# Two value projections from the unnormalised input, ahead of the norm

## The chip, the cores and the metric

The kernel runs on one core of a Trainium2 chip. The metric is the device time in microseconds of one execution; the runs of the kernel before have a median of 806.23 us.

## The reference

Two stacks of layers on x of 256 tokens and 1024 features, in float32. What is around the change is the first of them, an even layer:

```python
def rms_norm(x, g):
    xf = x.astype(f32)
    y = xf * lax.rsqrt(jnp.mean(xf * xf, axis=-1, keepdims=True) + EPS)
    return (y * g.astype(f32)).astype(x.dtype)

def even_layer(x, g_norm, w_in, b_f, w_out):
    z = rms_norm(x, g_norm) @ w_in
    qa, ka, va, ga, fa, qb, kb, vb, gb = jnp.split(z, cuts, axis=-1)
    log_f = jax.nn.log_sigmoid(fa.astype(f32) + b_f.astype(f32))
    ya = forgetting_attention(hA(qa), hA(ka), hA(va), log_f)   # 16 heads of 64, causal, decayed by cumsum(log_f)
    yb = dilated_attention(hB(qb), hB(kb), hB(vb))             # 16 heads of 64, three dilations
    y = jnp.concatenate([ya * jax.nn.silu(ga), yb * jax.nn.silu(gb)], axis=-1)
    return x + y @ w_out
```

Behind it come a retention layer with a norm and 4 heads, a layer with a state-space mixer beside sliding-window attention, and a gated feed-forward layer. Since the norm's factor is one number for each token, it can be multiplied on a product's rows instead of on x.

## The kernel before

All products are kept at float32 precision by splitting each operand into a high part (rounded to float32r) and a low part (the rest), and by three matmuls: high x high, high x low, low x high. The class `Weights` holds the list of all weight tiles (128 x 1024, 0.52 MB each) in the order in which they are used. `load` issues one tile's DMA on SP's queue into one of five raw buffers; `_prepare` casts it to the high part on ACT (L102) and takes the low part as a subtraction on DVE (L107), or on POOL for every n-th tile where a share is given to `plan`; `next` hands out a tile and prepares two ahead. The six pairs of prepared buffers hold what TensorE uses.

The start: x is loaded in two row tiles of two halves each (`load_x`), the gain row is spread over the partitions by TensorE (L636), and `norm_transposed` takes the squares (L232 on ACT, L229 on DVE), the factor (L217, L221 on POOL), multiplies x by factor and gain (L245), transposes on TensorE (L265), and splits into `xTh` and `xTl` (L272 on ACT, L273 on DVE). The second row tile's transposes are put behind the second matmul of the first product by `second_tile`. `first_xs` (L327, L334) is that first product, the v projection of the first eight forgetting heads: 48 matmuls of 512 columns.

Then the loop over the two kinds of heads (`m`: forgetting, dilated), two halves of eight heads (`hf`) and two groups of four heads (`i`): v by `proj_xs` (L312 to L316), the forget gates once (`forget_gates`, L281 to L283, a scan, and a store of the sums to DRAM at L678), then q, k and the gate by `proj_ws` (L293, L294; evacuated by ACT and DVE at L297 to L301), and for each pair of heads the scores (L376), masks read back from DRAM (`fox_masks`, L683 to L687), `masked_min` (L384, L386), exponentials, transposes (L400) and the product with v (L410). A product bank of kind `pp` exists three times, `at` twice, `pt` twice, `py` once. The tables of the state-space mixer (`tables_common`, L453 ff.) stand in the program behind the fourth group and are put earlier by the scheduler: each engine's instructions are laid out by a simulated timeline at build time, by priority and readiness, and then run in that order on the engine. On SP's queue the DMAs are in the same way in one fixed order.

Of the kernel before, what the change touches and what calls it, by code (L numbers as in the profile page):

```python
# [36 lines left out]
KE = ("pp", "py")  # L37
XH = 2
# [7 lines left out]
class Weights:  # L46


    def __init__(self, tc, raw, par, ahead):
        self.tc, self.nc, self.raw, self.par, self.ahead = tc, tc.nc, raw, par, ahead  # L50
        self.after, self.loaded, self.loads, self.lows = [], [], 0, []
        self.jobs, self.shares, self.done, self.used, self.ready = [], [], [], 0, {}

# [25 lines left out]
    def load(self):  # L79
        while self.loads in self.ready:  # L80
            self.loads += 1
        ap = self.jobs[self.loads]
        self.loads += 1
        r = self.raw.tile([P, 1024], F32, tag="raw", name="wraw")
        self.nc.sync.dma_start(r[:, :ap.shape[1]], ap)
        self.loaded.append(r)

    def _prepare(self):
# [13 lines left out]
        i = nc.scalar.copy(h[:, :n], r[:, :n])  # L102
# [5 lines left out]
        self.done.append((h, lo))  # L108

# [19 lines left out]
def model_kernel(ctx: ExitStack, tc: tile.TileContext, a: dict, out: bass.AP):  # L129
# [23 lines left out]
    g_row = nrm.tile([P, D], F32, tag="gain", name="g_row")  # L153
    nc.sync.dma_start(g_row[:1, :], a["even_norm"])
    x = [res.tile([P, D], F32, name=f"x{t}") for t in range(2)]

    def load_x(t):
        for h in range(XH):
            sl = slice(h * D // XH, (h + 1) * D // XH)
            nc.sync.dma_start(x[t][:, sl], a["x"][t * P:(t + 1) * P, sl])  # L160

    load_x(0)
# [9 lines left out]
    for m in ("a", "b"):  # L172
        for hf in range(2):
            w.plan(xs("w_v" + m, hf), SH[0] if m + str(hf) != "a0" else 2)
            if m == "a" and hf == 0:
                w.plan(ws("w_fa", 0))
# [24 lines left out]
    w.load()  # L201
    load_x(1)
# [32 lines left out]
    def norm_transposed(t, g, th, tl, name, kinds=("pt", "pt"), eng=None, after=None):  # L235

        with tc.high_priority():
            xt = x[t]
            parts = [mean_square(xt[:, h * 512:(h + 1) * 512], D, name, eng if h else None) for h in range(2)]
            r = rstd_from(parts, EPS, name)  # L240
            xn = []
            for h in range(2):
                sl = slice(h * 512, (h + 1) * 512)
                xn.append(nrm.tile([P, 512], F32, tag="xn", bufs=3, name="xn"))
                V.scalar_tensor_tensor(xn[h], xt[:, sl], r, g[h], op0=ALU.mult, op1=ALU.mult)  # L245
            return transposed(xn, 8, th, tl, 0, t, kinds, after)

# [11 lines left out]
    def transposed(src, n, th, tl, k0, t, kinds=("pt", "pt"), after=None):  # L259

        m = min(4, n)
        for b, sb, kind in zip(range(0, n, 4), src, kinds):
            pt = bank(kind)
            for j in range(m):
                i = T.transpose(pt[:, j * P:(j + 1) * P], sb[:, j * P:(j + 1) * P], ident)  # L265
                if after is not None:
                    tc.add_manual_dep(i.ins, after.ins.name, NOSYNC, reason="order")
                    after = None
# [49 lines left out]
    def first_xs(mid):  # L318

        tiles = [w.next() for _ in range(4)]  # L320
        ps = [bank("pp"), bank("pp")]
        for t in range(2):
            st = slice(t * P, (t + 1) * P)
            for g in range(0, 8, 2):
                for xp in (xTh, xTl):
                    for k in range(g, g + 2):
                        m = T.matmul(ps[t], xp[:, k, st], tiles[k // 2][0][:, 512 * (k % 2):512 * (k % 2) + 512],  # L327
                                     start=xp is xTh and k == 0, stop=False)
                        if t == 0 and xp is xTh and k == 1:
                            mid(m)  # L330
        for t in range(2):
            st = slice(t * P, (t + 1) * P)
            for k in range(8):
                T.matmul(ps[t], xTh[:, k, st], tiles[k // 2][1][:, 512 * (k % 2):512 * (k % 2) + 512],  # L334
                         start=False, stop=k == 7)
# [117 lines left out]
    def tables_common(pool, scratch):  # L453
# [7 lines left out]
        nc.sync.dma_start(sp, a["ssm_par"])  # L461
# [172 lines left out]
    g_even = [bank("at") for h in range(2)]  # L634
    for h in range(2):
        T.matmul(g_even[h], ones[:1, :], g_row[:1, h * 512:(h + 1) * 512], start=True, stop=True)  # L636
    norm_transposed(0, g_even, xTh, xTl, "e0", eng=V)

    def second_tile(after):
        norm_transposed(1, g_even, xTh, xTl, "e1", KE, None, after)  # L640

    lctx = ExitStack()
    ypool = lctx.enter_context(tc.tile_pool(name="ypool", bufs=1))
# [5 lines left out]
    yh, yl = y_tiles()  # L649
    with tc.tile_pool(name="ev", bufs=2) as ev, tc.tile_pool(name="evc", bufs=1) as evc, \  # L650
# [7 lines left out]
        def forget_gates():  # L658

            nc.sync.dma_start(bf, a["even_b_f"])  # L660
            nc.sync.dma_start(masks, a["c_masks"])
# [27 lines left out]

        for mi, m in enumerate(("a", "b")):  # L690
            for hf in range(2):
                ps = proj_xs(xTh, xTl, 8) if mi or hf else first_xs(second_tile)
                v = ev.tile([P, 2, 512], F32, tag="v", name="v")
                for t in range(2):
                    A.mul(v[:, t, :], ps[t], 0.5)
                if mi == 0 and hf == 0:
                    forget_gates()
                for i in range(2):
                    qk = []
# [3 lines left out]
                    proj_ws(k)  # L703
# [572 lines left out]
```

## Time and profile before

| | |
|---|---|
| runs, median | 806.23 us |
| profiled execution | 805.28 us, its span from first to last instruction 803.5 us |
| TensorE busy | 776.5 us (97%) |
| DVE, ACT, POOL busy | 592.8, 434.5, 202.0 us |
| granted TensorE clock, mean over the span | 0.992 |
| HBM | 162.9 MB moved, mean 203 GB/s |

The span is what the profile sees; the rest of the execution's time lies around it. Busy TensorE time is from pipelined matmuls whose ends are modelled, so that start-to-start distances say more of pace than durations do.

### The profile page before, as it was taken

How to read it: one execution, taken by the hardware profiler on the slowest of the kernel's cores; microseconds unless marked ns; L12 is line 12 of the kernel's file. 1: busy time of each engine (PE TensorE's matmuls, PEld its weight loads, DVE VectorE, ACT ScalarE, POOL GpSimd, SP SyncE). 2: the span in 40 equal slices, each digit the busy share in tenths (PEclk: the TensorE clock that was granted, in tenths of full speed). 3: DMA queues.
4: the chain of work that ended last, by engine and by line, in shares of the span. 5: the costliest groups of instructions: out<-in, count | busy, mean ns of one | idle time of the engine just before them, and what ended most of it. 6: DMA issues, size and time to landing. Idle time of an engine off the chain costs nothing.

```text
span 803.5 us, 12168 instructions
## 1 busy us (share of the span) xinstructions
PE 776.5 (97%) x4282; PEld 638.2 (79%) x4282; DVE 592.8 (74%) x1126; ACT 434.5 (54%) x783; POOL 202.0 (25%) x261
## 2 busy tenths in 40 slices
PE   7989999999999999999999999998898999999996
PEld 5867887877887778888888887796587888888886
DVE  7987677878888459796958666578759977786433
ACT  5875665665666347554444445627446655654431
POOL 4653111005405302201212003142233233223110
PEclk9999999999999999999999999999899999999999
DMA  8686553643844699985536395992333755555431
GB/s 296 215 276 231 170 171 119 222 153 123 270 163 146 199 337 388 358 288 196 192 123 210 123 323 177 326 357 93 124 124 110 238 192 184 183 185 183 157 131 53
DMA packets 55488, 162.91 MB, mean 203 GB/s; under 512 B 6385, under 2 KB 12801, under 8 KB 55426
## 3 DMA queue, kind: packets, MB, share of 16 engines
q1 hardware_dynamic: 55426, 162.12, 59.3%
q8 instruction: 34, 0.56, 0.3%
q14 instruction: 28, 0.23, 0.1%
HBM read 145.83 MB, written 16.27 MB: 202 GB/s over the span
## 4 chain that ended last, share of the span: by engine, by line
PE 83%; DVE 9%; DMA 3%; issue 3%; ACT 1%; SPq 0%; POOLq 0%; POOL 0%; DVEq 0%; ACTq 0%
PE bpp L293 19%; PE bpp L312 12%; PE bpp L313 12%; PE bpp L316 11%; PE bpp L294 10%; PE bat L293 5%; PE bat L294 2%; DVE wl L107 2%; PE bpy L410 2%; PE bpt L400 2%; PE bat L376 2%; DMA sr<-in_w_glu 1%; PE bat L955 1%; PE bpt L265 1%; DMA wraw<-in_w_v 1%
## 5 line engine op out<-in xcount | busy, mean ns | idle before, releaser
L107 DVE TENSOR_TENSOR wl<-wraw,wh 128x1024 fp32r<-128x1024 f32 x214 | 272.2, 1287 | 89.7 <-ACT wh L102 89.3
L102 ACT CAST wh<-wraw 128x1024 fp32r<-128x1024 f32 (+1 forms) x225 | 230.9, 1045 | 123.2 <-PE bpp L316 38.8
L293 PE MATMUL bpp<-xT,wh 128*128 128x512 f32 x672 | 242.6, 402 | 4.1 <-DVE q L301 4.1
L294 PE MATMUL bpp<-xT,wl 128*128 128x256 f32 x672 | 191.1, 284 | 0.0
L293 PEld LDWEIGHTS bpp<-xT,wh 128*128 128x128 f32 x672 | 126.9, 189 | 35.2 <-DVE q L301 4.7
L294 PEld LDWEIGHTS bpp<-xT,wl 128*128 128x128 f32 x672 | 127.6, 190 | 1.9 <-issue 1.2
L313 PE MATMUL bpp<-wl,xT 128*128 128x512 f32 (+1 forms) x288 | 109.4, 385 | 2.4 <-DVE wl L107 2.4
L312 PE MATMUL bpp<-wh,xT 128*128 128x512 f32 (+1 forms) x288 | 110.1, 389 | 0.1
L316 PE MATMUL bpp<-wh,xT 128*128 128x512 f32 (+1 forms) x288 | 75.3, 383 | 0.5 <-DVE xT L365 0.5
L313 PEld LDWEIGHTS bpp<-wl,xT 128*128 128x128 f32 x288 | 54.8, 190 | 13.6 <-DVE wl L107 3.8
L312 PEld LDWEIGHTS bpp<-wh,xT 128*128 128x128 f32 x288 | 54.6, 190 | 12.8 <-issue 1.5
L316 PEld LDWEIGHTS bpp<-wh,xT 128*128 128x128 f32 x288 | 52.2, 189 | 11.3 <-DVE xT L365 0.9
L293 PE MATMUL bat<-xT,wh 128*128 128x512 f32 x160 | 57.1, 399 | 0.0
L312 PE MATMUL bpp<-wh,yh 128*128 128x512 f32 x128 | 50.5, 400 | 0.0
L313 PE MATMUL bpp<-wl,yh 128*128 128x512 f32 x128 | 50.3, 396 | 0.0
L107 POOL TENSOR_TENSOR wl<-wraw,wh 128x1024 fp32r<-128x1024 f32 x11 | 27.4, 2492 | 85.5 <-ACT wh L102 85.5
L294 PE MATMUL bat<-xT,wl 128*128 128x256 f32 x160 | 45.0, 281 | 0.0
L293 PEld LDWEIGHTS bat<-xT,wh 128*128 128x128 f32 x160 | 30.1, 188 | 7.4
L316 PE MATMUL bpp<-wh,yl 128*128 128x512 f32 x128 | 35.7, 398 | 0.0
L393 ACT ACTIVATE s<-s,nm 128x128 f32<-128x128 f32 x40 | 15.8, 396 | 27.9 <-DVE nm L384 20.2
L294 PEld LDWEIGHTS bat<-xT,wl 128*128 128x128 f32 x160 | 30.2, 189 | 0.0
L1158 POOL TENSOR_TENSOR gr<-gr,Rh 128x512 f32<-128x512 f32 x10 | 19.8, 1980 | 38.4 <-ACT th L1157 38.4
(392 smaller groups left out, 1285.7 us busy)
## 6 DMA issues: line engine op xcount, KB each, us to landing
wraw<-in_w_o SPq DMA_DIRECT2D x36, 512.0 KB, 4.3
wraw<-in_w_gate SPq DMA_DIRECT2D x22, 512.0 KB, 3.7
wraw<-in_w_up SPq DMA_DIRECT2D x22, 512.0 KB, 3.4
wraw<-in_w_dn SPq DMA_DIRECT2D x22, 512.0 KB, 4.0
wraw<-in_w_v SPq DMA_DIRECT2D x16, 512.0 KB, 5.6
wraw<-in_w_g SPq DMA_DIRECT2D x16, 512.0 KB, 4.8
wraw<-in_w_q SPq DMA_DIRECT2D x12, 512.0 KB, 4.9
wraw<-in_w_va SPq DMA_DIRECT2D x8, 512.0 KB, 6.0
```

The lines of the kernel that those rows point to most:

```text
L102: i = nc.scalar.copy(h[:, :n], r[:, :n])
L107: self.lows.append(eng.tensor_tensor(lo[:, :n], r[:, :n], h[:, :n].bitcast(F32), op=ALU.subtract))
L293: T.matmul(ps, h, xT2[:, k].rearrange("p a b -> p (a b)"), start=k == 0, stop=False)
L294: T.matmul(ps[:, :S], l, xTh[:, k, :], start=False, stop=k == 7)
L312: T.matmul(ps, lh[:, k0 + k, st], wh, start=first and k == 0, stop=False)
L313: T.matmul(ps, lh[:, k0 + k, st], wl, start=False, stop=False)
L316: T.matmul(ps, ll[:, k0 + k, st], wh, start=False, stop=last and k == n - 1)
L376: i = T.matmul(ps[j][:, o], q[rows, qs], k[rows, ks], start=True, stop=True)
L393: A.activation(p[:, :P], s[:, :P], AF.Exp, bias=nm[:, 0:1], scale=-1.0, accum_out=dn[:, 0:1])
L400: T.transpose(pt[:, j * P:(j + 1) * P], p[:, j * P:(j + 1) * P], ident)
L410: i = T.matmul(o[64 * j:64 * j + 64], v[:, b, vc], src, start=b == 0, stop=b == 1)
L1158: G.tensor_tensor(two(gr), two(gr), rep2(Rh), op=ALU.mult)
```

## The change

x comes in a second time, transposed on the host (`xT`, eight blocks of 128 features by 256 tokens), and the even gain as a column for each block. The unnormalised, gained blocks are split at once into `xuh` and `xul` (in the buffer that later holds y's high part). Both v projections of the forgetting heads are computed from them: `first_xs` for the first half, group by group as blocks and weights arrive, then `proj_xs` for the second half in the banks of kind `at`; their evacuation multiplies by the factor of each token (`rh`, with the 0.5 that stood there before). Meanwhile `normalised` sums squares over the blocks, reduces them over the partitions with two small matmuls, spreads the factors over the partitions with two more, and writes the normalised `xTh` and `xTl` for the gates, q, k, g and the dilated heads' v. The first four weight tiles go into the buffer of y's low part, so nine raw tiles can be in flight; the first of them is loaded and cast in two halves. Three matmuls on ones run before anything has landed. x itself, the masks and the state-space parameters are issued later. All splits of these first weights are DVE's.

```diff
+        if self.loads in self.given:
+            r = self.given.pop(self.loads)
+        else:
+            r = self.raw.tile([P, 1024], F32, tag="raw", name="wraw")
+        parts = 2 if self.loads == 0 else 1
...
+        if not self.done:
+            nc.scalar.copy(h[:, :n // 2], r[:, :n // 2])
+            i = nc.scalar.copy(h[:, n // 2:n], r[:, n // 2:n])
...
+    def issue_after(self, n, i):
+
+        self.tc.add_manual_dep(i.ins, self.issued[n].ins.name, NOSYNC, reason="order")
...
+    warm = bank("py")
+    for n in (4, 4, 2):
+        T.matmul(warm[:, :n * P].rearrange("p (a b) -> p a b", a=n), ones, ones[:, None, :].to_broadcast([P, n, P]),
+                 start=True, stop=True)
+    warm = const.tile([P, 1], F32, name="warm")
+    A.copy(warm, ones[:, :1])
...
     def load_x(t):
...
+        w.issue_after(10, nc.sync.dma_start(x[t], a["x"][t * P:(t + 1) * P, :]))
...
-            w.plan(xs("w_v" + m, hf), SH[0] if m + str(hf) != "a0" else 2)
-            if m == "a" and hf == 0:
+            if m == "b":
+                w.plan(xs("w_vb", hf), SH[0])
+            elif hf == 0:
+                for h in range(2):
+                    w.plan(xs("w_va", h), SH[0])
                 w.plan(ws("w_fa", 0))
...
+    xu = ypool.tile([P, 16, S], F32R, tag="yh", name="xu")
+    xuh, xul = (xu.rearrange("p (k j) s -> p k j s", j=2)[:, :, j, :] for j in range(2))
+    early = ypool.tile([P, 16, S], F32R, tag="yl", name="early")[:].rearrange("p a b -> p (a b)").bitcast(F32)
+    w.given = {j: early[:, 1024 * j:1024 * j + 1024] for j in range(4)}
+    w.between = lambda: load_xT(1, 1)
+    for k in (2, 4, 6):
+        w.load()
+        load_xT(k)
+    for _ in range(5):
+        w.load()
...
-    def norm_transposed(t, g, th, tl, name, kinds=("pt", "pt"), eng=None, after=None):
...
+    def first_xs():
+
+
         ps = [bank("pp"), bank("pp")]
...
+        for g in range(0, 8, 2):
+            tiles.append(w.next())
+            part(g, xuh, 0, first=g == 0)
+            part(g, xul, 0)
+            if g:
+                part(g - 2, xuh, 1)
+        part(6, xuh, 1, last=True)
         return ps
...
-        nc.sync.dma_start(sp, a["ssm_par"])
+        w.issue_after(12, nc.sync.dma_start(sp, a["ssm_par"]))
...
-    g_even = [bank("at") for h in range(2)]
-    for h in range(2):
-        T.matmul(g_even[h], ones[:1, :], g_row[:1, h * 512:(h + 1) * 512], start=True, stop=True)
-    norm_transposed(0, g_even, xTh, xTl, "e0", eng=V)
...
+    for k in range(8):
+        xk = xT[k // 4][:, k % 4, :]
+        A.activation(xuh[:, k, :], xk, AF.Copy, scale=g_col[:, k:k + 1])
+        V.scalar_tensor_tensor(xul[:, k, :], xk, g_col[:, k:k + 1], xuh[:, k, :].bitcast(F32),
+                               op0=ALU.mult, op1=ALU.subtract)
...
+        def square_sums():
+
+            sq = [ev.tile([P, 512], F32, tag=n, name="sq_e") for n in ("q", "k", "q", "k")]
+            for j in range(4):
+                A.activation(sq[j], xT[j // 2][:, 2 * (j % 2):2 * (j % 2) + 2, :].rearrange("p a b -> p (a b)"),
+                                 AF.Square, scale=1.0 / math.sqrt(D))
...
+        def normalised():
+
+            sm = square_sums()
+            pr = bank("pt")
...
+                T.matmul(pr[:, t:t + 1], sm[:, t * P:(t + 1) * P], ones[:, :1], start=True, stop=True)
...
+                V.tensor_copy(rb, rs[t].to_broadcast([P, P]))
+                T.matmul(pr[:, t * P:(t + 1) * P], rb, ident, start=True, stop=True)
+            A.copy(R, pr[:, :S])
...
+            for k in range(8):
+                xk = xT[k // 4][:, k % 4, :]
+                V.scalar_tensor_tensor(xk, xk, g_col[:, k:k + 1], R, op0=ALU.mult, op1=ALU.mult)
+                if k % 2:
+                    xk = xT[k // 4][:, k % 4 - 1:k % 4 + 1, :]
+                    split(xTh[:, k - 1:k + 1, :], xTl[:, k - 1:k + 1, :], xk)
+            return rh
+
         for mi, m in enumerate(("a", "b")):
             for hf in range(2):
-                ps = proj_xs(xTh, xTl, 8) if mi or hf else first_xs(second_tile)
...
+                if first:
+                    ps = first_xs()
+                    with tc.high_priority():
+                        rh = normalised()
+                    ps = [ps, proj_xs(xuh, xul, 8, ps=[bank("at"), bank("at")])]
+                    yh, yl = y_tiles()
+                    va = [ev.tile([P, 2, 512], F32, tag="v", name="v") for _ in range(2)]
+                    for h in range(2):
+                        for t in range(2):
+                            A.mul(va[h][:, t, :], ps[h][t], rh[t])
                     forget_gates()
...
+                    if first and not i:
+                        w.issue_after(6, nc.sync.dma_start(masks, a["c_masks"]))
+                        for t in range(2):
+                            load_x(t)
...
+    a["xT"] = c(a["x"].T.reshape(8, P, S).transpose(1, 0, 2))
+    a["even_norm"] = c(i["even_norm"][0].reshape(8, P).T)
```

## Rows read from the trace of the kernel before

**Rows 1.** The page: busy time of TensorE, and the chain that ended last.
```profile
PE 776.5 (97%) x4282; PEld 638.2 (79%) x4282; DVE 592.8 (74%) x1126; ACT 434.5 (54%) x783; POOL 202.0 (25%) x261
...
PE 83%; DVE 9%; DMA 3%; issue 3%; ACT 1%; SPq 0%; POOLq 0%; POOL 0%; DVEq 0%; ACTq 0%
```

**Rows 2.** Waits of TensorE, whole run: who, for whom; us in total, times, longest.
```profile
PE bpp L293 <- DVE q L301: 4.1, 2, 3.3
```

**Rows 3.** Instructions in order of time, 6 to 13 us: start, duration, instruction.
```profile
6.86 1.05 ACT L102 CAST wh<-wraw 128x1024 fp32r<-128x1024 f32 x1 [2.35 <-DMA wraw<-in_w_va]
7.87 0.63 ACT L232 ACTIVATE junk<-x 128x512 bf16<-128x512 f32 x1
9.77 2.08 PE L327 MATMUL bpp<-wh,xT 128*128 128x512 f32 x4 [0.46 <-ACT xT L272]
11.22 2.38 POOL L107 TENSOR_TENSOR wl<-wraw,wh 128x1024 fp32r<-128x1024 f32 x1 [1.15 <-ACT wh L102]
12.27 2.42 DVE L107 TENSOR_TENSOR wl<-wraw,wh 128x1024 fp32r<-128x1024 f32 x1
```

**Rows 4.** TensorE in order of time, 21 to 26 us.
```profile
21.27 2.44 PE L334 MATMUL bpp<-wl,xT 128*128 128x512 f32 x10
23.54 0.28 PE L281 MATMUL bpp<-xT,wh 128*16 128x256 f32 x1
...
25.95 0.40 PE L293 MATMUL bpp<-xT,wh 128*128 128x512 f32 x1
```

**Rows 5.** Stretches: length, busy time by engine, granted clock, DMA share, GB/s.
```profile
core 0: us, PE busy (x) PEld busy (x) DVE busy (x) ACT busy (x) POOL busy (x), PEclk, DMA share, GB/s
17.70:26.00 8.30, 8.30 (x50) 6.59 (x49) 8.13 (x42) 6.39 (x9) 1.56 (x4) 1.00 0.74 266
36.00:40.00 4.00, 3.29 (x19) 2.58 (x18) 4.00 (x11) 3.01 (x6) 3.94 (x3) 1.00 0.00 0
62.00:64.00 2.00, 2.00 (x8) 1.71 (x7) 2.00 (x4) 0.00 (x0) 2.00 (x3) 0.50 0.90 324
80.00:120.00 40.00, 40.00 (x238) 32.57 (x237) 29.18 (x72) 25.41 (x55) 4.86 (x5) 1.00 0.52 172
```

**Rows 6.** Groups by shape, TensorE, 10.5 to 13 us, then 17 to 19 us: busy, mean ns.
```profile
L327 PE MATMUL bpp<-wh,xT 128*128 128x512 f32 x6 | 3.0, 628 | 0.5 <-ACT xT L272 0.5
...
L327 PE MATMUL bpp<-wh,xT 128*128 128x512 f32 x6 | 1.5, 389 | 0.0
```

**Rows 7.** Stretches of the start, columns as in rows 5.
```profile
2.30:7.30 5.00, 3.75 (x4) 1.14 (x4) 2.37 (x9) 1.16 (x3) 1.20 (x5) 1.00 0.96 313
7.30:13.00 5.70, 5.20 (x18) 4.21 (x19) 5.28 (x8) 5.06 (x10) 2.33 (x2) 1.00 0.98 383
```

**Rows 8.** Groups by shape, DVE, 26 to 50 us: busy us, mean ns of one.
```profile
L107 DVE TENSOR_TENSOR wl<-wraw,wh 128x1024 fp32r<-128x1024 f32 x10 | 12.1, 1209 | 0.0
L427 DVE SCALAR_TENSOR_TENSOR trig<-trig 128x512 f32<-128x512 f32 x6 | 4.0, 670 | 0.0
...
L301 DVE SCALAR_TENSOR_TENSOR q<-bpp,q 128x256 f32<-128x256 f32 x3 | 1.2, 404 | 0.0
...
L520 DVE TENSOR_TENSOR sm_t<-pw_r 128x32 f32<-128x32 f32 x1 | 0.2, 207 | 0.0
```

**Rows 9.** Groups, ACT, 26 to 45 us.
```profile
L102 ACT CAST wh<-wraw 128x1024 fp32r<-128x1024 f32 x7 | 7.2, 1047 | 3.4 <-PE bpp L293 2.2 <-DMA wraw<-in_w_ga 1.1
...
L300 ACT ACTIVATE q<-bpp 128x256 f32<-128x256 f32 x2 | 0.8, 379 | 0.6 <-PE bpp L294 0.6
```

**Rows 10.** The masks' way through DRAM and what stood behind it, in order of time.
```profile
44.42 0.32 SPq L678 DMA_DIRECT2D c_dram<-c_f  x1
...
53.09 0.73 POOL L686 TENSOR_TENSOR m<-m,masks 128x256 f32<-128x256 f32 x1 [3.52 <-DMA m<-c_dram]
...
53.86 0.29 DVE L384 CUSTOM_DVE_ANT_0 s<-bat,m 128x128 f32<-128x128 f32 x1 [3.48 <-POOL m L686]
...
60.56 0.41 DVE L301 SCALAR_TENSOR_TENSOR q<-bpp,q 128x256 f32<-128x256 f32 x1
...
61.03 0.80 PE L293 MATMUL bpp<-xT,wh 128*128 128x512 f32 x1 [3.34 <-DVE q L301]
```

**Rows 11.** TensorE in order of time: the second v projection's first matmul.
```profile
69.71 0.50 PE L312 MATMUL bpp<-wh,xT 128*128 128x512 f32 x1
```

## What I expected before the changed kernel ran

> **What bounds the kernel now.** I read the page's busy times and chain of waits first. TensorE is busy 776.5 of 803.5 us, and the chain that ended last runs through it for 83% of the span [rows 1]. So time is won only where TensorE stands still or runs slowly, or where it gets less work. Next the waits of TensorE over the whole run: the largest named wait inside the stage that the diff touches is for the evacuation of a q product (two waits, 4.1 us in all, the longer 3.3 us) [rows 2]. Then the first 26 us in order of time. TensorE's first product of the kernel starts at 9.77 us: the x tile must land, be squared, be scaled and be transposed before that [rows 3]. From there the first v projection and the 24 small matmuls of the forget gates last until 25.95 us, when the q projection begins [rows 4]. From then on the two waits for q are the only ones up to 64 us, and from 80 to 120 us TensorE is busy all 40.00 us [rows 5]. A gain at the start is therefore kept to the end unless one of those waits grows.
>
> The first matmuls are also slow: six 128x512 matmuls between 10.5 and 13 us average 628 ns, six of the same shape between 17 and 19 us average 389 ns [rows 6]. That is 0.24 us more each, and it is what a matmul shows where the granted clock is 0.50, the 1.2 GHz level [rows 5]. The granted-clock column says 1.00 in the early stretch [rows 7], so I take the durations and not that column.
>
> **The change, in one comparison point.** I compare the moment at which the q projection can start. Before, it is 25.95 us. In the changed kernel the second v projection (48 matmuls) stands ahead of it too, and is missing later, so the moment to beat is 25.95 plus 48 matmuls. Ten matmuls of that projection's shape take from 21.27 to 23.54 us, 0.227 us from start to start [rows 4]; 48 take 10.9 us. The moment to beat is 36.85 us.
>
> **Removed.** Sixteen transposes, their eight evacuations (ACT and DVE), the gain broadcast on TensorE, and the chain square, rstd, scale, transpose, split ahead of the first product. Also the share of weight splits that POOL took: beside one of them (2.38 us from 11.22 us) DVE's own split lasted 2.42 us [rows 3] against a mean of 1.209 us later [rows 8]. They go to DVE, two more splits, 2.4 us.
>
> **When data lands now.** The queue order becomes gain column, xT 0 (0.13 MB), half of w 0 (0.26), xT 1 (0.13), other half, xT 2-3 (0.26), w 1 (0.52), xT 4-5, w 2, xT 6-7, w 3 to w 7. The queue moved 313 GB/s from 2.30 to 7.30 us and 383 GB/s from 7.30 to 13.00 us [rows 7]. In the kernel before, 1.05 MB were ahead of and in the first weight tile; at that rate they are through at 5.6 us, and ACT starts its cast at 6.86 us [rows 3], so landing is seen 1.3 us later. With the same rates and lag: first half of w 0 (0.39 MB) at 4.8 us, second half (0.79 MB) at 6.0, w 1 (1.57 MB) at 8.5, w 2 (2.36 MB) at 10.6, w 3 (3.15 MB) at 12.7, w 7 (5.24 MB) about 18. A cast of a whole tile takes 1.05 us [rows 9].
>
> **TensorE's start.** First matmul at 4.8 + 0.55 = 5.35 us. The first group (8 matmuls) ends near 7.5 us; then TensorE waits for w 1, cast at 9.55 us: a new wait of 2 us. From there each group of 12 matmuls takes 2.7 us against 2.1 us between landings, so it never waits for weights again: 12 + 12 + 12 + 4 matmuls end at 18.6 us, the 48 of the second v projection at 29.5 us. The four small matmuls of the norm I put at 0.8 us (nothing if they run in the 2 us gap's place, 2 us if TensorE stands in order before them until the sums are ready). The gates' 24 matmuls start 0.115 us apart (23.54 to 25.95 us for 21 of them) [rows 4]: 2.8 us. The q projection starts at 33.1 us. Gain 36.85 - 33.1 = 3.7 us. All eight matmuls of the first group at once and no norm stall would make it 5.5 us; the 2 us norm stall and a landing 1 us later make it 1.5 us.
>
> **DVE under it.** Until the gates, DVE must do eight low halves of xu (128x256, 0.404 us), eight weight splits (1.209 us), and the norm chain: three adds and four splits of 512 columns (0.67 us), one add and eight scalings of 256 columns (0.404 us), six tiny ones of some 0.2 us [rows 8]. That is 3.2 + 9.7 + 4.7 + 3.6 + 1.2 = 22.4 us; from 5 us on it ends at 27.4 us, and the gates want its result at 30.3 us. A margin of 2.9 us: the norm is hidden under the second v projection, though not by much. ACT has 8 casts (8.4 us), 8 scalings of 0.38 us [rows 9], four squares of 0.63 us [rows 3], a copy and four splits: under 18 us in the same time, so it doesn't bind.
>
> **Moved on the queue.** x is now loaded once more (1 MB), behind the q weights; masks and the state-space parameters are issued later as well. At 36 to 40 us the queue moved nothing [rows 5], so 1 MB (3 us of it) is hidden there. x is wanted only at the output projection. The masks' late load is covered by the gates' own chain, whose DRAM round trip is not through before 53 us [rows 10]. Each of these I cost at nothing.
>
> **The second v's old place.** It stood at 69.71 us, among the first softmax chains [rows 11]. The q, k and g projections of the next half move up in its place, with two buffers each for q and k, so I cost its loss as a filler at nothing; bound from above by the 3.3 us wait of the same stage.
>
> **Sum.** 805.28 us profiled - 3.7 = 801.6 us. The median of the runs shown is 0.95 us above the profiled execution: 802.5 us.
>
> **Clock, row and rule.** The three early matmuls on ones keep TensorE busy until the first landing, which should take the low level off the first products; that is in the 3.7 us. The row shows 0.24 us more for each matmul at the low level [rows 6], and after TensorE's 3.3 us wait at 57.7 us a stretch of granted clock 0.50 [rows 5]. The Trainium skill (TensorE: Matmul & The Clock Gate, "What's actually happening") says that the array is throttled by default and that sustained activity, not a number of matmuls, releases it; an idle stretch puts it back. By that rule the wait for w 1 could undo the early matmuls; the next paragraph prices this from the rows.
>
> **Rivals.**
> - *The start stays at the low clock.* The 2 us wait, or a late release, leaves some 12 matmuls at 1.2 GHz: 12 x 0.24 = 2.9 us. For it: the wait of 3.3 us did this [rows 5]. Against: 2 us is shorter. Gain 0.8 us, 805.4 us.
> - *The mask wait goes too.* Before, DVE stood in order for the masks from 50.3 to 53.86 us; behind it the q evacuation came only at 60.56 us and TensorE stood until 61.03 us [rows 10]. The wait costs 3.3 us and some 1.5 us of low clock behind it. With the tables' work out of its way, the gates' chain may now come early against the projections. Against: the DMA round trip in it (44.42 to 53.09 us) is untouched. 802.5 - 4.8 = 797.7 us.
> - *Other side: the tables' work comes back in the wrong place.* The state-space parameters are issued behind twelve weight tiles. From 17.7 to 26 us DVE was busy 8.13 us, of which the weight splits are some 2.7 us (two at 1.22 us and the begin of a third); the other 5.4 us are the tables' small work. It must now run later, into a stretch where DVE is full (4.00 of 4.00 us from 36 to 40 us) [rows 5]. If it stands ahead of an evacuation, TensorE waits for the product bank as it did at 57.7 us. From 3.7 us of such waits on there is no gain; with all 5.4 us the time is 802.5 + 5.4 = 808 us. For it: a full DVE and the two waits for q [rows 2]. Against: this work isn't due in the stage, and DVE has room later (29.18 of 40.00 us from 80 to 120 us) [rows 5].
> - *The norm is not hidden.* The sign turns only if the gates' operands are 2.9 + 3.7 = 6.6 us later than summed; I leave that inside the previous case's chance.
>
> **Numbers.** Forecast 0.46 (800 to 804), low clock 0.15 (804 to 806.5), mask wait gone 0.17 (796 to 800), slower or no gain 0.19 (806 to 809); 0.03 for schedules turned over elsewhere, by more than 2% either way. Range 796 to 809, with about 0.1 outside. Two per cent is 16 us, about what a measurement of this kernel can tell from no change. The upper bound of the start (5.5 us), both waits for q (4.1 us) and the low clock behind the second (1.5 us) are together 11 us, so faster than that has 0.01; slower by as much needs several new waits like the longest, 0.02. Within: 0.97.
>
> **What would show it.** Right: TensorE's first v matmul near 5.4 us at about 0.39 us each, a wait near 8 us for a cast of w 1, the first q matmul between 31.5 and 35 us, the chain at TensorE there. Wrong: first q matmul after 36.85 us, with the wait ahead of the gates put to DVE (norm late); matmuls of 0.63 us up to 12 us (clock); a wait for a q or k evacuation over 3.3 us between 35 and 75 us (tables).

## The result, and the profile after

The changed kernel takes 811.75 us (median of 14 runs, 807.33 to 817.31) beside 806.09 us for the kernel before; the ratio is 1.0089, with a 95% interval of 1.0067 to 1.011: some 7 us lost where 3.7 were expected to be won. The time lies above the range of the prediction, and on the other side of the kernel before. The profiled execution is one of the longer ones, 815.72 us with a span of 813.9.

The page first, the lines that answer to [rows 1]:

```profile
PE 782.1 (96%) x4276; PEld 641.2 (79%) x4276; DVE 598.4 (74%) x1146; ACT 438.1 (54%) x792; POOL 195.5 (24%) x259
...
PE 82%; DVE 8%; DMA 4%; ACT 3%; issue 2%; POOL 1%; SPq 0%; POOLq 0%; DVEq 0%; ACTq 0%
```

TensorE has as good as the same number of matmuls, is busy 5.6 us longer for them, and the span has grown by 10.4 us: the rest is standing. On the chain that ended last POOL now has 1%. The waits of TensorE, as in [rows 2], say where it stands:

```profile
PE bat L404 <- DVE nm L414: 4.9, 1, 4.9
...
PE bpp L353 <- ACT wh L115: 2.7, 1, 2.7
...
PE bpp L308 <- DVE xT L393: 1.9, 1, 1.9
PE bpp L319 <- DVE q L327: 1.8, 2, 1.5
```

Three of the four are new. The longest is at the scores, which wait for a bank of kind `at` that DVE's `masked_min` hasn't emptied; the next two are in the start; only the last is the wait for q of [rows 2], shorter than it was. Then the stretches (columns as in [rows 5]):

```profile
2.00:4.00 2.00, 2.00 (x4) 0.90 (x3) 0.75 (x4) 0.49 (x2) 0.91 (x6) 1.00 0.77 206
4.00:6.00 2.00, 2.00 (x4) 0.93 (x4) 0.48 (x1) 1.40 (x4) 0.00 (x0) 1.00 0.67 200
...
12.00:14.00 2.00, 2.00 (x7) 1.57 (x8) 1.85 (x3) 2.00 (x5) 0.00 (x0) 0.75 1.01 412
14.00:16.00 2.00, 2.00 (x6) 1.55 (x5) 1.90 (x3) 2.00 (x5) 0.00 (x0) 0.50 1.04 420
...
60.00:80.00 20.00, 13.66 (x64) 10.82 (x62) 12.81 (x31) 9.33 (x18) 10.46 (x11) 0.83 0.57 185
```

DMA moved 206 and 200 GB/s from 2 to 6 us, against the 313 of [rows 7]. The granted clock fell to its lower level (0.50) at 14 to 16 us, and again in the stretch from 60 to 80 us, where TensorE is busy only 13.66 of 20 us.

**The start**, TensorE in order of time (compare [rows 3, 4]):

```profile
5.48 1.04 PE L353 MATMUL bpp<-wh,xu 128*128 128x512 f32 x2
7.45 1.66 PE L353 MATMUL bpp<-wh,xu 128*128 128x512 f32 x6 [0.92 <-ACT wh L113]
11.85 2.84 PE L353 MATMUL bpp<-wh,xu 128*128 128x512 f32 x8 [2.74 <-ACT wh L115]
14.49 1.91 PE L353 MATMUL bpp<-wl,xu 128*128 128x512 f32 x4
...
34.91 0.28 PE L307 MATMUL bpp<-xT,wh 128*16 128x256 f32 x1
37.06 0.29 PE L308 MATMUL bpp<-xT,wh 128*16 128x256 f32 x1 [1.87 <-DVE xT L393]
```

The first product starts on time, waits 0.92 us for the second half of the first weight tile and 2.74 us for the next tile, and then four matmuls take 1.91 us where later ones take 1.09. Both v projections end at 34.9 us; a gate matmul then waits 1.87 us for the normalised x. From 34.91 us, with this wait and the 2.8 us that the prediction has for the gates' 24 matmuls, the point at which q's share of the work begins is 39.6 us, 2.7 us behind the 36.85 us to beat. (The gates stand among the q matmuls now, so the first q matmul, at 37.78 us, can't be compared.) Why the second tile was late (its DMA on SP's queue, with size and time from issue to landing, then ACT):

```profile
3.52 0.43 SPq L91 DMA_DIRECT2D early<-in_w_va  x1
...
early<-in_w_va SPq DMA_DIRECT2D x1, 512.0 KB, 7.2
```
```profile
9.36 0.63 ACT L717 ACTIVATE sq_e<-xT 128x512 f32<-128x512 f32 x1 [1.97 <-DMA xT<-in_xT]
9.90 0.89 ACT L666 ACTIVATE xu<-xT,g_col 128x256 fp32r<-128x256 f32 x2
10.76 1.04 ACT L115 CAST wh<-early 128x1024 fp32r<-128x1024 f32 x1
```

The tile was issued at 3.52 us and landed at 10.7 us, and ACT cast it at 10.76 us. Ahead of it in ACT's order stood x blocks 2 and 3, which came at 9.36 us; their squares and scalings were done just as the tile landed, so ACT's order cost next to nothing here.

**The masks.** Their way through DRAM, all engines in order of time (compare [rows 10]):

```profile
52.57 0.67 DVE L698 TENSOR_TENSOR_SCAN c_f<-ones,z_f 16x256 f32<-16x256 f32 x1
...
53.04 2.82 POOL L596 COPY m<-sm_mag 128x256 f32<-128x256 f32 x1 [0.71 <-DMA w_dram<-m]
...
55.80 1.52 POOL L557 COPY rv_r<-pw_r 128x16 f32<-128x16 f32 x1
...
57.31 0.95 POOL L558 COPY rv_i<-pw_i 128x16 f32<-128x16 f32 x1
...
58.19 4.51 POOL L700 COPY c_f<-c_f 16x256 f32<-16x256 f32 x1
...
62.10 0.41 DVE L324 TENSOR_TENSOR gp<-bpp,gp 128x256 f32<-128x256 f32 x1
...
62.73 0.32 SPq L701 DMA_DIRECT2D c_dram<-c_f  x1
...
68.94 0.72 POOL L709 TENSOR_TENSOR m<-m,masks 128x256 f32<-128x256 f32 x1 [6.24 <-DMA m<-c_dram]
69.70 0.29 DVE L412 CUSTOM_DVE_ANT_0 s<-bat,m 128x128 f32<-128x128 f32 x1 [7.19 <-POOL m L709]
...
71.89 1.66 PE L404 MATMUL bat<-k,q 64*128 64x128 f32 x8 [4.86 <-DVE nm L414]
```

The scan that makes the sums is done at 53.2 us. The copy that prepares its store stands on POOL behind three copies of the state-space tables (L596, L557, L558), starts 5 us later, and takes 4.51 us; the store is issued 9.5 us after the scan. DVE then stands 7.19 us for the first mask. From the scan's start to the first `masked_min` are 17.1 us; before, they were 10.8 us (from the scan at 43.03 us to the `masked_min` in [rows 10]). All of the delay lies ahead of the store: from the store to the first addition on POOL are 6.2 us here and were 8.7 us before. The scan itself is 9.5 us later than before.

The POOL copy's 4.51 us go with DVE: DVE worked without a gap from the scan to 62.51 us, mostly two-input operations, and the copy ended 0.2 us after it. The Trainium skill (SBUF — State Buffer, "SBUF: two separate sides") says that VectorE and GpSimd share one pair of ports, which whoever comes first holds exclusively, a VectorE operation with two inputs from SBUF included. This row agrees; the same copy takes 0.64 us in the kernel before and 0.65 to 2.65 us in the other kernels where POOL has it. No run isolates the ports as the reason.

The first matmul of the first output projection (the product with `yh`) starts at 252.18 us instead of 243.58. Of these 8.6 us, TensorE's idle time up to 240 us gives 5.0 (13.25 against 8.26 us, by the stretches).

### The profile page after: what moved, and what is told of

It reads as the page before. It is cut to its first block, busy times and chain, and to the rows that moved or that the text cites. A ratio compares the mean times of both kernels' runs of the same rounds, so it can differ in the third digit from the quotient of the medians.

```text
span 813.9 us, 12195 instructions
## 1 busy us (share of the span) xinstructions
PE 782.1 (96%) x4276; PEld 641.2 (79%) x4276; DVE 598.4 (74%) x1146; ACT 438.1 (54%) x792; POOL 195.5 (24%) x259
## 4 chain that ended last, share of the span: by engine, by line
PE 82%; DVE 8%; DMA 4%; ACT 3%; issue 2%; POOL 1%; SPq 0%; POOLq 0%; DVEq 0%; ACTq 0%
PE bpp L319 18%; PE bpp L338 11%; PE bpp L339 11%; PE bpp L342 11%; PE bpp L320 9%; PE bat L319 5%; PE bat L320 2%; DVE wl L121 2%; PE bpy L438 2%; DMA sr<-in_w_glu 2%; PE bpt L428 2%; PE bat L404 2%; PE bpp L353 1%; PE bat L339 1%; PE bat L338 1%
## 5 line engine op out<-in xcount | busy, mean ns | idle before, releaser
L121 DVE TENSOR_TENSOR wl<-wraw,wh 128x1024 fp32r<-128x1024 f32 (+1 forms) x212 | 268.9, 1283 | 87.1 <-ACT wh L115 84.7
L115 ACT CAST wh<-wraw 128x1024 fp32r<-128x1024 f32 (+1 forms) x221 | 226.3, 1044 | 121.4 <-PE bpp L342 39.2
L339 PE MATMUL bpp<-wl,xT 128*128 128x512 f32 (+1 forms) x272 | 103.2, 385 | 2.0 <-DVE wl L121 2.0
L338 PE MATMUL bpp<-wh,xT 128*128 128x512 f32 (+1 forms) x272 | 103.8, 389 | 0.4 <-ACT wh L115 0.3
L342 PE MATMUL bpp<-wh,xT 128*128 128x512 f32 (+1 forms) x272 | 71.2, 384 | 0.5 <-DVE xT L393 0.5
L339 PEld LDWEIGHTS bpp<-wl,xT 128*128 128x128 f32 x272 | 51.7, 190 | 12.9 <-DVE wl L121 3.5
L338 PEld LDWEIGHTS bpp<-wh,xT 128*128 128x128 f32 x272 | 51.5, 190 | 11.6 <-issue 1.2
L342 PEld LDWEIGHTS bpp<-wh,xT 128*128 128x128 f32 x272 | 49.2, 189 | 11.2 <-DVE xT L393 0.9
L121 POOL TENSOR_TENSOR wl<-wraw,wh 128x1024 fp32r<-128x1024 f32 x9 | 22.5, 2495 | 83.6 <-ACT wh L115 83.6
```

What stands on the lines that cost most here:

```text
L121: self.lows.append(eng.tensor_tensor(lo[:, :n], r[:, :n], h[:, :n].bitcast(F32), op=ALU.subtract))
L338: T.matmul(ps, lh[:, k0 + k, st], wh, start=first and k == 0, stop=False)
L339: T.matmul(ps, lh[:, k0 + k, st], wl, start=False, stop=False)
L342: T.matmul(ps, ll[:, k0 + k, st], wh, start=False, stop=last and k == n - 1)
```

## The experiments

Line numbers shift by up to four among the kernels; ratios are to the kernel before, run beside each.

**The place of the state-space parameters.** The theory after the first reading was that the tables' work, which begins when the parameters land, had moved between scan and masks. Two kernels move it out, one to each side; one changes only the copy's engine; one moves the parameters in the kernel before.

`e1_params_early`, the changed kernel with
```diff
-        w.issue_after(12, nc.sync.dma_start(sp, a["ssm_par"]))
+        nc.sync.dma_start(sp, a["ssm_par"])
```


> The changed kernel with one part undone: the state-space parameters are loaded without the order behind twelve weight tiles. Pool theory (the loss is the tables' small POOL work, pushed by that order in front of POOL's copy of the gate sums, whose store to DRAM came 10.2 us after the scan against 1.4 us before): the tables run some 10 us earlier, the store comes 2 to 6 us earlier against the scan, TensorE's 4.9 us wait ahead of the second scores shrinks below 3 us, time 806 to 809 us. Rival, start theory (the loss is the late landing, the low clock and the norm ahead of the gates; the masks' wait is what it was before): the parameters' 0.57 MB and the tables' DVE work come ahead of the norm, so nothing is won or 1 to 2 us are lost, 811 to 814 us.

806.55 us, ratio 0.9997 (0.9975 to 1.0019). `e3_params_late` has `issue_after(24` instead of 12:

> The changed kernel with the state-space parameters issued behind weight tile 24 instead of 12, so that the tables' work on POOL and DVE comes after the first masks. Pool theory: the store is issued within 2 us of the scan and nothing of the tables stands between the masks' landing and their additions, the 4.9 us wait goes, 803 to 807 us. Start theory: 811 us within 1 us, and any tables' work that comes later may cost more.

805.64 us, ratio 1.0008 (0.9987 to 1.003). Either way the loss is gone, and so is the wait at the scores. In the kernel with the early load:

```profile
52.01 0.67 DVE L698 TENSOR_TENSOR_SCAN c_f<-ones,z_f 16x256 f32<-16x256 f32 x1
...
53.80 1.32 POOL L700 COPY c_f<-c_f 16x256 f32<-16x256 f32 x1
...
62.50 0.29 DVE L412 CUSTOM_DVE_ANT_0 s<-bat,m 128x128 f32<-128x128 f32 x1 [1.34 <-POOL m L709]
```

and in the one with the late load, where the parameters are issued after the sums were stored:

```profile
48.80 1.51 POOL L700 COPY c_f<-c_f 16x256 f32<-16x256 f32 x1 [22.09 <-DVE c_f L698]
...
58.31 0.29 DVE L412 CUSTOM_DVE_ANT_0 s<-bat,m 128x128 f32<-128x128 f32 x1
58.70 0.43 SPq L489 DMA_DIRECT2D ssm_par<-in_ssm_par  x1
```

From scan to `masked_min` are 10.5 and 10.3 us again (the late kernel's scan starts at 47.99 us). So the order behind twelve tiles costs 1.0089 - 1.0008, or some 6.5 us. That the scan is late isn't what costs: in the kernel with the early load it comes at 52.01 us, nearly as late as in the changed kernel.

`e2_copy_on_dve`, the changed kernel with
```diff
-            G.tensor_copy(c2.rearrange("p (t j c) -> p t c j", t=2, j=4), natural(c))
+            V.tensor_copy(c2.rearrange("p (t j c) -> p t c j", t=2, j=4), natural(c))
```


> The changed kernel with POOL's reordering copy of the gate sums on DVE, right behind the scan there. Pool theory: the store to DRAM is issued within 1.5 us of the scan instead of 10.2 us, the masks land some 8 us earlier, the 4.9 us wait and the low clock behind it go, 804 to 807 us. Start theory: the masks were not the cause, 811 us within 1 us.

810.98 us, ratio 1.0091 (1.0057 to 1.0125): nothing won, against the pool theory's 804 to 807 us. The copy takes 0.42 us on DVE, but behind the tables' operations and the weight splits it comes only 4.6 us after the scan at 49.73 us:

```profile
54.35 0.42 DVE L700 COPY c_f<-c_f 16x256 f32<-16x256 f32 x1
...
54.47 6.13 POOL L558 COPY rv_i<-pw_i 128x16 f32<-128x16 f32 x1
...
55.94 0.38 SPq L701 DMA_DIRECT2D c_dram<-c_f  x1
...
60.06 1.29 SPq L706 DMA_DIRECT2D m<-c_dram  x3
...
64.33 0.73 POOL L709 TENSOR_TENSOR m<-m,masks 128x256 f32<-128x256 f32 x1 [2.88 <-DMA m<-c_dram]
...
65.09 0.29 DVE L412 CUSTOM_DVE_ANT_0 s<-bat,m 128x128 f32<-128x128 f32 x1 [3.37 <-POOL m L709]
...
74.10 0.80 PE L319 MATMUL bpp<-xT,wh 128*128 128x512 f32 x1 [5.88 <-DVE q L327]
```

15.4 us from scan to `masked_min`, and the wait turned into 5.9 us for a q evacuation, the kind that the prediction's rival had named. So the slow POOL copy isn't the cause by itself: the tables' work in this place delays the masks on either engine, and TensorE pays at the scores or at q. What holds the masks back after the store here is the way through DRAM: the store, behind two weight tiles on the queue, takes 4.1 us to land (1.4 us in the changed kernel), the reads go out only then, and POOL, done with its table copies at 61.45 us, waits 2.88 us for them.

`e4_before_params_later`, the kernel before with
```diff
-        nc.sync.dma_start(sp, a["ssm_par"])
+        w.issue_after(8, nc.sync.dma_start(sp, a["ssm_par"]))
```


> The kernel before with that part of the change alone: the state-space parameters issued behind its weight tile 8 (the same place in its list, counted from the first q tile). If the later tables alone bring the loss, whatever the start does, it is 4 us or more slower than the kernel before, 810 us or above. Pool theory, by the order on POOL in this build (the copy of the gate sums stands ahead of most of the tables' copies): within 2 us of the kernel before. Start theory: the same as the kernel before.

803.74 us, ratio 0.9985 (0.9959 to 1.0011), no difference. There POOL copies the sums right behind the scan (at 37.76 us), ahead of the tables' copies, and `masked_min` starts at 49.38 us. Later parameters alone hurt nothing. Nor is it how near they land to the scan: 14 us ahead of it here, 18 us ahead of it in the changed kernel. What hurts is the laid-out order, in which the tables' work stands between the scan and the store. Why the build put it there in the changed kernel and not here, no run shows.

**The start.** With the parameters out of the way the forecast gain was still missing. These four are edits of the kernel with the late load (ratio 1.0008).

`s1_act_queue`, both loads of x's column form on ACT's queue:
```diff
-    nc.sync.dma_start(g_col, a["even_norm"])
+    nc.scalar.dma_start(g_col, a["even_norm"])
...
-        nc.sync.dma_start(xT[k // 4][:, k % 4:k % 4 + n, :], a["xT"][:, k:k + n, :])
+        nc.scalar.dma_start(xT[k // 4][:, k % 4:k % 4 + n, :], a["xT"][:, k:k + n, :])
```


> The changed kernel with late tables (e3), and with the gain column and the xT blocks issued from ACT's queue, the weights alone on SP's. Issue theory (the first 6 us moved only 200 GB/s against 263 to 314 before, because eleven DMAs, many of them small, are issued one by one 0.47 us apart): w 1 lands 1.5 to 2 us earlier, the 2.7 to 3.2 us wait for its cast shrinks below 1.5 us, the low clock behind it goes, 2 to 4 us faster than e3 (805.6), 801.5 to 803.5 us. Rival, landing is bound by the transfer itself: the wait stays within 0.5 us, time within 1 us of e3.

813.08 us, ratio 1.0113 (1.0086 to 1.0141): slower, against both expectations. SP now issued the first four weight tiles by 4.0 us, and the first two blocks of x were both there only at 8.75 us (5.34 us in the changed kernel):

```profile
8.75 0.63 ACT L717 ACTIVATE sq_e<-xT 128x512 f32<-128x512 f32 x1 [6.11 <-DMA xT<-in_xT]
...
10.74 5.49 PE L353 MATMUL bpp<-wh,xu 128*128 128x512 f32 x12 [5.07 <-ACT wh L112]
```

ACT, in order, squares and scales these blocks ahead of its first cast, so that TensorE starts at 10.74 us, and then runs its first products 0.43 us or more apart, the pace of the low level. The reading is that the single queue had rationed the weights, and that without it they took the DMA engines. The Trainium skill (DMA: Bandwidth & Descriptors, "Issuing engines are not separate DMA queues") says that DMAs issued by ScalarE, SyncE or GpSimd run on the same 16 DMA engines and interleave there; the trace agrees: x blocks 0 and 1, issued from 1.22 us on with only the small gain column ahead of them on their queue, were both there 7.5 us later.

`s2_whole_loads`, first weight tile and x blocks 0 and 1 in one DMA each, the tile cast whole:
```diff
-        parts = 2 if self.loads == 0 else 1
+        parts = 1
...
-        if not self.done:
-            nc.scalar.copy(h[:, :n // 2], r[:, :n // 2])
-            i = nc.scalar.copy(h[:, n // 2:n], r[:, n // 2:n])
-        else:
-            i = nc.scalar.copy(h[:, :n], r[:, :n])
+        i = nc.scalar.copy(h[:, :n], r[:, :n])
...
-    load_xT(0, 1)
+    load_xT(0)
```


> The late-tables kernel (e3) with the first weight tile loaded and cast whole and xT 0 and 1 in one DMA: nine DMAs instead of eleven up to w 3. Issue theory: the first matmul comes 1.5 us later, w 1 lands about 0.9 us earlier, the gap ahead of w 1 closes by 2 us or more and the clock stays up; 0 to 2 us faster than e3. Rival (the early start is worth what it gives): 1 to 2 us slower than e3.

801.04 us, ratio 0.9972 (0.9945 to 0.9999): 0.36% less than with the loads split, with intervals that overlap a little. From 4 to 6 us the DMA engines move 356 GB/s (a stretch, columns as in [rows 5]):

```profile
4.00:6.00 2.00, 1.67 (x3) 0.43 (x2) 0.63 (x2) 1.43 (x3) 0.00 (x0) 1.00 0.96 356
```

and TensorE in order of time begins with

```profile
7.76 6.75 PE L349 MATMUL bpp<-wh,xu 128*128 128x512 f32 x16 [2.09 <-ACT wh L111]
```

The first product starts 2.4 us later than with the loads split (5.37 us), but from there the projection waits for no weights. This profiled execution, 805.93 us, is one of the longer ones of its kernel.

`s3_no_warm`, without the three matmuls on ones:
```diff
-    for n in (4, 4, 2):
-        T.matmul(warm[:, :n * P].rearrange("p (a b) -> p a b", a=n), ones, ones[:, None, :].to_broadcast([P, n, P]),
-                 start=True, stop=True)
```


> The late-tables kernel (e3) without the three matmuls on ones. If they keep the clock up for the first products: the first eight matmuls run at 0.43 us instead of 0.23 us, hidden for the most part in the wait for w 1; TensorE then starts the long stretch at the low level as it does with them (e3 has a granted clock of 0.79 from 12 to 20 us). I expect within 1 us of e3. Rival (they are worth the 2.9 us that the prediction gave them): 2 to 3 us slower than e3.

808.44 us, ratio 1.0051 (1.0025 to 1.0076): by the centres they are worth some 3.5 us (the intervals just overlap), more than the 1 us expected, and near the 2.9 us that the prediction put on a low clock at the start. The number agrees, but the trace doesn't show that way:

```profile
7.38 5.53 PE L349 MATMUL bpp<-wh,xu 128*128 128x512 f32 x14 [0.74 <-ACT wh L113]
...
35.59 0.39 PE L304 MATMUL bpp<-xT,wh 128*16 128x256 f32 x1 [3.01 <-DVE xT L389]
```

The first products are slow without the matmuls on ones, but the gates begin at 32.29 us, 3.1 us sooner than in the trace of the late kernel, where the second weight tile landed late; here they wait 3.01 us for the normalised x. What the matmuls on ones save, and where, stays open.

`s4_spread_early`, the matmuls that spread the factors (L740, at 30.96 us in the changed kernel though their operand is there at 26.5) ordered behind the 11th matmul of the second v projection:
```diff
+                i = T.matmul(ps, lh[:, k0 + k, st], wh, start=first and k == 0, stop=False)
+                if spread and k == 3:
+                    tc.add_manual_dep(i.ins, spread.pop().ins.name, NOSYNC, reason="order")
...
+                sp_ = T.matmul(pr[:, t * P:(t + 1) * P], rb, ident, start=True, stop=True)
+            spread.extend([sp_, sp_])
```


> The late-tables kernel (e3) with the matmuls that spread the norm's factor put on TensorE's queue behind the 11th matmul of the second v projection instead of the 33rd. Order theory (the norm is late because these two matmuls stood in TensorE's order behind matmuls that ran late; their operand was ready at 26.5 us and they ran at 30.96): the normalised x is ready some 4 us earlier, the gates' 1.9 us wait and the broken start of q go, 2 us faster than e3, 803 to 804 us. Rival (DVE's own work sets the norm's end): the wait shrinks by less than 0.7 us, time within 1 us of e3.

805.17 us, ratio 1.0015 (0.9996 to 1.0033): the wait ahead of the gates is gone from the trace, and the time is as it was. The order theory has the wait right, the rival the time.

**Do the causes add?** Four kernels with the whole loads. `t1_whole_spread` adds the edit of `s4_spread_early`; `t2_whole_early` issues the parameters early; `t3_whole_only` keeps them behind 12 tiles; `t4_whole_longwarm` has `for n in (4, 4, 4, 2):` matmuls on ones, to close the gap ahead of the first product.

> The changed kernel with the whole first loads alone; the state-space parameters stay behind 12 tiles. Theory A (two separate causes that add): the loads give back some 4.6 us as they did with the parameters behind 24 tiles, 811.75 - 4.6 = about 807 us, and the wait for the masks' minimum stays at 4 to 5 us. Rival B (one cause: the late start is what puts the tables' work between the scan and the masks): about 801 us, no mask wait.

808.81 us, ratio 1.0051 (1.0027 to 1.0074). The loads give 0.38% (3.1 us) with the parameters in the wrong place, as they gave 0.36% without. Each pair of intervals overlaps a little, but both pairs agree, as two causes that add would have it; the place of the parameters costs 0.79% with whole loads (1.0051 against 0.9972) and 0.81% with split ones. The price of that place only moved, to a wait of 4.10 us for a q evacuation, behind DVE's stand for the masks (13.3 us from scan to `masked_min`):

```profile
72.26 0.80 PE L315 MATMUL bpp<-xT,wh 128*128 128x512 f32 x1 [4.10 <-DVE q L323]
```

> Whole first loads, and the state-space parameters issued at the start again, as in the kernel before, instead of behind 24 tiles. Theory A (any place of the parameters that keeps the tables' work from standing between the gates' scan and the masks is as good as another; loads of the start are a separate term): the same as with the parameters behind 24 tiles, 800 to 803 us, no mask wait. Rival B (DVE needs the tables' work away from the start): 804 us or more, with a longer wait for q.

805.06 us, ratio 0.9992 (0.9968 to 1.0017). This is the rival's figure: with whole loads the parameters behind 24 tiles are better by the centres (0.9972, and 0.9951 and 0.9955 in the two kernels below) than early ones, though the interval reaches into those of all three. Early parameters put the tables' work back beside the projections, and a q wait of 3.0 us stays, as in the kernel before.

> Whole first loads, parameters behind 24 tiles, and a fourth group of matmuls on ones (14 blocks of 128 columns instead of 10), so that TensorE is busy until about 7.5 us, when the first weight tile's cast is ready, instead of 5.7 us. Theory A (after the 2.1 us gap the first 16 products ran at the 1.2 GHz level, 6.75 us for 16 or 0.42 us each, against 0.23 us later): without the gap the 16 take about 4 us, gain up to 2.9 us at the first products, and 1.5 to 2.5 us at the end: 798.5 to 799.5 us. Rival B (the first products are held by the arrival of weights and x, not by the clock): they end at the same time, 801 us.

802.16 us, ratio 0.9955 (0.993 to 0.9979): not the 798.5 to 799.5 us of theory A, and the interval overlaps with that of the shorter warming, so no gain is shown. The profiled executions say why. The same first products, in `s2_whole_loads` (above), and here in `t3_whole_only`, `t2_whole_early`, `t1_whole_spread` and `t4_whole_longwarm`, in this order:

```profile
7.41 4.40 PE L349 MATMUL bpp<-wh,xu 128*128 128x512 f32 x16 [1.74 <-ACT wh L111]
```
```profile
6.87 4.40 PE L349 MATMUL bpp<-wh,xu 128*128 128x512 f32 x16 [1.20 <-ACT wh L111]
```
```profile
6.70 2.13 PE L353 MATMUL bpp<-wh,xu 128*128 128x512 f32 x8 [1.32 <-ACT wh L111]
```
```profile
6.72 2.13 PE L349 MATMUL bpp<-wh,xu 128*128 128x512 f32 x8 [0.30 <-ACT wh L111]
```

In `s2_whole_loads` sixteen matmuls take 6.75 us, 0.42 us each, the pace of the low level, which the granted-clock column doesn't show there (the prediction met the same in [rows 6, 7]). In the others they run at the full pace, 0.23 us apart; the 4.40 us hold a short wait for the second tile in the middle. From execution to execution the same start begins between 6.70 and 7.76 us, and the low level shows in one of the five traces. The shorter warming already gets the full pace in `t1_whole_spread`, and the sixteen are through at 11.01 us there and at 11.16 us with the longer one: the arrival of the second tile decides, as rival B says.

> The kernel with whole first loads (first weight tile and first two blocks of x in one DMA each, state-space parameters behind 24 tiles; 801.04 us measured), and now the two matmuls that spread the factors ordered behind the 11th matmul of the second v projection. Theory A (waits at the start add up on the path that ends last): the 1.9 us wait ahead of the gates goes and stays gone, about 799 us. Rival B (what is won at the gates is given back at the q evacuations, as with the loads split): same as before it, 800.5 to 802 us.

801.17 us, ratio 0.9951 (0.9926 to 0.9976), the fastest by ratio, some 3.9 us under the kernel before, and rival B's figure rather than theory A's 799 us. In its trace the first gate matmul starts at 31.41 us without a wait:

```profile
31.41 0.28 PE L303 MATMUL bpp<-xT,wh 128*16 128x256 f32 x1
31.53 0.28 PE L304 MATMUL bpp<-xT,wh 128*16 128x256 f32 x1
```

With 2.8 us for the gates that is 34.2 us, 2.6 us ahead of the moment to beat. The spreading itself isn't shown to bring it: the intervals of the three kernels with whole loads and late parameters overlap.

## Why the prediction was wrong

**The view was right.** TensorE bounds the kernel, and the places that decided are the two that the prediction looked at: the start and the stretch from 50 to 80 us.

**The step that failed first: "each of these I cost at nothing".** The paragraph on what moves on the queue took masks and parameters together and covered them by the gates' DRAM round trip. It asked when the bytes land, not what work their landing releases and what stands behind that work. The parameters release the tables' work on DVE, ACT and POOL; behind it, in order, stands the copy that opens that same round trip, on POOL or on DVE. So the cover was itself what was delayed: 17.1 us from scan to `masked_min` instead of 10.8. Price: 6.5 us.

**The rival on the other side was nearly it.** "The tables' work comes back in the wrong place" had the cause and the wait for a bank, at 0.19 and up to 808 us. It looked at DVE's 5.4 us and at the evacuation of q; in the changed kernel it was POOL's order, the masks and a bank of kind `at`, and with the DVE copy, or whole loads, it was q after all. Its "against" (this work isn't due in the stage, DVE has room later) failed: the laid-out order put the work into the stage all the same. The bound of 5.4 us left out the low clock behind the wait and POOL's share.

**The second step: when data lands.** 313 GB/s and a lag of 1.3 us were taken from a start with larger transfers. With small ones issued 0.47 us apart the queue moved some 203 GB/s from 2 to 6 us, and 290 GB/s from 6 to 10 us where the sum had 383 from 7.3 us on. At these rates the 1.57 MB up to the second tile are through at 8.6 us instead of 7.2, and the tile landed 2.1 us behind that instead of 1.3: by 10.7 us the queue had moved 2.25 MB, so transfers issued after the tile had moved beside it. TensorE got it at 11.85 us, not 9.55: 2.3 us. From there to 23.29 us stand 42 matmuls (40 of the first v, two of the second) in 11.44 us; at 0.2335 us from start to start, as later in the same projection, they take 9.8: 1.6 us for the low level of the clock, the rival that had 0.15. The pace itself, against the 0.227 us of [rows 4], is 0.6 us over both projections. Together 4.5 of the 4.6 us by which the gates begin late (34.91 against 30.3 us); with the 1.87 us of wait ahead of them the gain of 3.7 us is a loss of 2.7.

These are sizes of one execution, 4 us longer than the median, and they scatter. With the loads split and the matmuls on ones, the first sixteen products are through between 12.20 us (`e2_copy_on_dve`, the gates at 32.56 us) and 15.01 us (the kernel with the late load), 14.49 us here. With whole loads it is 11.01 to 11.65 us in four traces and 14.35 us in the fifth.

**The norm under the second v** was hidden on DVE in the sum, but not in TensorE's order: the matmuls that spread the factors came 4.4 us after their operand was ready, and the scalings after them. Removing this wait alone moved nothing that could be measured, so its price isn't shown.

**What held.** The price of a product but for 3%, and the first matmul at 5.48 us (5.35). The worth of the matmuls on ones came out near 2.9 us in the time alone; with its way not in the trace, this may be luck. The rival "the mask wait goes too" came true once the parameters were out of the way: with the late load no wait for a mask or for q is left until 95 us, where one of 1.31 us stands. The two waits of [rows 2] and the slow stretch behind (4.1 + 1.5 us), less this 1.31, are a gain of 4.3 us. Its late start (first gate at 35.36 us, and 1.87 us of wait: 3.2 us behind the moment to beat) took most of that back. The 1.1 us that are left fit this profiled execution (804.41 against 805.28 us), and a ratio of 1.0008 can't tell them from nothing.

**Open** is what share of the whole loads' gain is the rate (356 GB/s instead of 200 to 270 from 4 to 6 us), what the clock and what the cast's place: the edit changes all three, and no run takes them apart.

## What to carry to other kernels

When a load is moved, ask what work its landing releases, on which engines, and what stands behind that work in order; "the bytes are hidden" prices only the bytes. A chain through DRAM has short steps on several engines, and each of them can be queued behind work that nobody waits for. At a start, sum landings by the number and size of the transfers and by what moves beside them, not by bytes alone, and then follow the engine that handles them in order.

## What the runs showed of the hardware that was not expected

A POOL copy of 16x256 took 0.64 us in the kernel before and 4.51 us beside a DVE that was busy without a gap, one of 128x16 took 0.19 us and as much as 6.13 us (spans on POOL are rough, but the store behind the 4.51 us bears it out). After a gap of TensorE the granted clock isn't told by the gap's length alone: 2.74 us was followed by the low level in the changed kernel, and in `s4_spread_early` a gap of 2.73 us at nearly the same place was followed by eight matmuls in 2.13 us, at full pace. And a second issuing queue made the first two blocks of x land later, 8.75 us instead of 5.34, not sooner.
